# One pool for two projection stages, and smaller splitting steps for attention's weight tiles

## The chip, the cores and the metric

The kernel runs on one core of a Trainium2 chip. Its time is the device time of the whole program in microseconds; the number for a kernel is the median over its runs. A core has five instruction queues that run side by side: TensorE (PE, with its weight loads as PEld), VectorE (DVE), ScalarE (ACT), GpSimd (POOL) and SyncE (SP), the last of which only issues transfers here. Each queue is worked off in order. Whatever an instruction needs from another queue it waits for with a semaphore, and everything behind it on its own queue waits too.

## The reference

One decoder layer on a 1024 x 1024 input in float32: adaptive RMS norm, one wide input projection, a stick-breaking attention branch, a multi-scale causal pooling branch, two sigmoid gates that join them, and an output projection with a final norm.

```
h = rms_norm(x, norm_gain) * (1 + scale) + shift
q, k, v, z_a, u, z_b, m_a, m_b = split(h @ w_in)

z = q @ k.T * 64 ** -0.5                      # 16 heads of 64, s < t only
A[t, s] = sigmoid(z_ts) * prod over s < j < t of (1 - sigmoid(z_tj))
p_a = (concat_heads(A @ v) * silu(z_a)) @ w_branch_a
p_b = (pool(u) * silu(z_b)) @ w_branch_b

merged = sigmoid(m_a) * p_a + sigmoid(m_b) * p_b
out = rms_norm(x + gate * (merged @ w_out), final_gain)
```

## The kernel before

Every matrix product is made in three passes. An operand is split into a high half, the operand rounded to the type that PE reads (`F32R`), and a low half, the rest; the product is high x high, high x low and low x high, summed in one PSUM bank. The high half comes from a cast on ACT (`act.copy`), the low half from a subtraction on DVE or POOL. `h`, split and transposed, stays in SBUF as `hT` for the whole first part.

The stages follow each other on PE in this order: the pooling input `u`; the values `v` (tiles `vp`); the joining gate `m_b` (tiles `mp`); the gate of the pooling branch `z_b` (tiles `wzb`); the pooling branch's product (tiles `bp`); attention, in which the remaining projections (tiles `p`: k, q, z_a, m_a) are mixed with the heads' own work; and the last products (`pa`, `o`).

**Values and joining gate** are both made by `seven` (line 565 on), which forms a 2 x 2 block product from seven block products instead of eight, in the order p1, p5, p6, p7, p4, p3, p2, each of 48 matmuls. Its operands are weight blocks, loaded by the function that the caller hands in (line 679 for values, 697 for the gate), some of which are first added or subtracted on DVE: `a_s1` loads `a21` into a weight buffer and `a22` into a buffer of tag `ar`, adds them (line 576), loads `a11` into the other `ar` buffer and keeps the difference in `s2k` (line 578). `a_op` (lines 547 to 549) splits the result, `b_op` (lines 553 to 555) splits sums of `h` blocks into tiles of tag `bhl`. Banks are copied out by ACT (line 598) or added to by DVE (line 562). Finished values are split (lines 685 and 686) and stored to DRAM (line 687); finished gates go through a sigmoid (line 701) and are stored (line 702).

Tiles come out of pools. A tag is a ring of `bufs` buffers that all tiles of that tag share. `vs` and `ms` are two pools on the right side of SBUF, opened and closed one after the other, so `ms` lies on the bytes that `vs` had; the sizes of their last tags differ, so equal tags do not lie on equal bytes. `raw` and `whl` (the loaded and the split weights) are in the pool `wts`, which is open all the time and has two buffers of each.

**Attention** works on 64 units of one head and 256 queries. For a block row of queries PE makes the logits `z`, ACT writes `om` and `be` from them (two sigmoids, lines 921 and 922), POOL puts ones and zeros on the diagonal block of each (line 926), DVE runs a product scan along `om` (line 928) and multiplies it onto `be`. PE transposes blocks of `be` into a bank, ACT and DVE split them into `wt` (lines 947 and 948), and PE multiplies them with the values (`av`). Between these, PE works off the projection tiles: 32 weight tiles of 128 x 1024, each with 48 matmuls `p`. `load_parts` (line 138) loads and splits such a tile through `load_w` (line 127) and `split` (line 112): one cast of 128 x 1024 on ACT (line 121), and one subtraction of 128 x 1024 on POOL (line 116; on DVE for the tile number `MASKED`). Both of the two `raw` and `whl` buffers are in use, so a tile is split when the matmuls of the tile two before it are done. SP issues the loads of the tiles (line 129) in one queue with the moves of q and k between partitions (line 799) and the stores of attention's result (line 978).

What sets the order on the queues: PE's order from attention on is the order of the program (`pinned`), and so is that of some instructions on the other engines. All the rest is ordered by a planner when the program is built. It goes through a simulated run and issues whatever is ready on a free queue, earlier program lines first. In the pools with `reuse_waits="tile"` an instruction waits only for the tiles that lay on its own bytes.

Of the kernel before, what the change touches and what calls it, by code (L numbers as in the profile page):

```python
# [9 lines left out]
F32 = mybir.dt.float32  # L10
F32R = mybir.dt.float32r
AF = mybir.ActivationFunctionType
ALU = mybir.AluOpType
PSUM = bass.MemoryType.PSUM

P = 128
D = 1024
S = 1024
KB = D // P
# [17 lines left out]
MASKED = 4  # L37

HD = 64
# [12 lines left out]
def block_kernel(ctx, tc, a, out):  # L52
    nc = tc.nc
    v, act, gp = nc.vector, nc.scalar, nc.gpsimd

    def pool(name, **kw):
        return tc.tile_pool(name=name, bufs=1, reuse_waits="tile", **kw)
# [69 lines left out]
    def load_w(src, name, hi_eng, lo_eng):  # L127
        raw = wts.tile([P, KB, P], F32, tag="raw", bufs=2, name=name + "_raw")
        nc.sync.dma_start(raw.rearrange("p k c -> p (k c)"), src)
        return split(raw, [P, KB, P], wts, "whl", 2, hi_eng, lo_eng, name)  # L130
# [5 lines left out]
        tiles += [CK + p, CQ + p] + [gates.pop(0) for _ in range(GATES[p])] + [CZA + p]  # L136
    tiles += gates
    def load_parts(i, name):
        return load_w(a["w_in"][tiles[i]], name, act, v if i == MASKED else gp)

    def mm3(ps, whl, mhl, kbs, mov, first=True, last=True):
        (wh, wl), (mh, ml) = whl, mhl
# [38 lines left out]
    with pool("init") as init:  # L181
# [30 lines left out]
        def load(dst, src):  # L212
            tc.keep_in_program_order(nc.sync.dma_start(dst, src))
# [338 lines left out]
    def b_op(src, pl, bufs, name):  # L552
        hl = pl.tile([P, 2, 2, 512], F32R, tag="bhl", bufs=bufs, name=name)
        act.copy(hl[:, 0], src)
        v.tensor_sub(hl[:, 1], src, hl[:, 0].bitcast(F32))
        return lambda m, e: hl[:, m, e]

    def k2(t, q):
        return t[:, 2 * q:2 * q + 2]
# [4 lines left out]

    def seven(nm, sums, load, b_of, a_moves, ta, tb, final, direct):

        s2k = sums.tile([P, 4, 512], F32, name=nm + "s2k")

        def raw(first, m, k, q, name):
            t = (wts if first else sums).tile([P, 2, 512], F32, tag="raw" if first else "ar", bufs=2, name=f"{nm}{name}_{q}")  # L570
            load(t, m, k, q)
            return t

        def a_s1(q):
            r, w = raw(1, 1, 0, q, "a21"), raw(0, 1, 1, q, "a22")
            v.tensor_add(r, r, w)
            w = raw(0, 0, 0, q, "a11s")
            v.tensor_sub(k2(s2k, q), r, w)
            return r

        def a_s3(q):
            r, w = raw(1, 0, 0, q, "a11d"), raw(0, 1, 0, q, "a21d")
            v.tensor_sub(r, r, w)
            return r

        def a_s4(q):
            r = raw(1, 0, 1, q, "a12s")
            v.tensor_sub(r, r, k2(s2k, q))
            return r

        a_of = dict(
            p1=lambda q: raw(1, 0, 0, q, "a11"), p5=a_s1, p6=lambda q: k2(s2k, q), p7=a_s3,
            p4=lambda q: raw(1, 1, 1, q, "a22"), p3=a_s4, p2=lambda q: raw(1, 0, 1, q, "a12"),
        )

        def copied(tag, bufs, j, src):
            t = sums.tile([P, 512], F32, tag=tag, bufs=bufs, name=f"{nm}{tag}_{j}")
            act.copy(t, src)
            return t

        chain, keep = {}, {}
        for name in ("p1", "p5", "p6", "p7", "p4", "p3", "p2"):
            c = {"p5": "b", "p3": "b", "p2": "c"}.get(name, "a")
            if c not in chain:
                chain[c] = [bank((tb if c == "b" else ta)[j // 2], f"{nm}{name}_{j}") for j in range(4)]
            ps = chain[c]
            for q in range(2):
                al, bl = a_op(a_of[name](q), f"{nm}{name}a{q}"), b_of(name, q)
                for j in range(4):
                    js = slice(j * P, j * P + P)  # L610
                    for e in range(2):
                        for i, (w, m) in enumerate(((0, 0), (0, 1), (1, 0))):
                            l, r = (bl(m, e)[:, js], al[:, w, e]) if a_moves else (al[:, w, e, js], bl(m, e))
                            mm(
                                ps[j], l, r, start=name in ("p1", "p5", "p2") and (q, e, i) == (0, 0, 0),
                                stop=(q, e, i) == (1, 1, 2), skip_group_check=True,
                            )
            for j in range(4):
                if name == "p1":
                    keep["s1", j] = copied("s1", 4, j, ps[j])  # L620
                elif name == "p6":
                    keep["s2", j] = copied("s2", 4, j, ps[j])
                elif name == "p7":
                    final(1, 1, j, added(copied("s3", 4, j, ps[j]), chain["b"][j]))
                elif name == "p4":
                    final(1, 0, j, ps[j] if direct else copied("s3", 4, j + 4, ps[j]))
                elif name == "p3":
                    final(0, 1, j, added(keep["s2", j], ps[j]))
                elif name == "p2":
                    final(0, 0, j, added(keep["s1", j], ps[j]))  # L630

    with pool("vp") as vp:

        tq = [vp.tile([P, 4, 512], F32, name=f"ht{i}") for i in range(4)]

        def hq(k, n, q):
            sl = slice(4 * k + 2 * q, 4 * k + 2 * q + 2), slice(512 * n, 512 * n + 512)
            return [t[:, sl[0], sl[1]].bitcast(F32) for t in (h_hi, h_lo)]

        def difference(dst, x, y, name):  # L640
            tmp = vp.tile([P, 2, 512], F32, tag="tmp", bufs=1, name=name)
            v.tensor_sub(dst, x[0], y[0])
            v.tensor_sub(tmp, x[1], y[1])
            v.tensor_add(dst, dst, tmp)

        def without(dst, x, y):
            v.tensor_sub(dst, x[0], y)
            v.tensor_add(dst, dst, x[1])

        def make_t(i, q):  # L650
            dst = k2(tq[i], q)
            if i == 0:
                difference(dst, hq(0, 1, q), hq(0, 0, q), f"tmp0_{q}")
            elif i == 1:
                without(dst, hq(1, 1, q), k2(tq[0], q))
            elif i == 2:
                difference(dst, hq(1, 1, q), hq(0, 1, q), f"tmp2_{q}")
            else:
                without(dst, hq(1, 0, q), k2(tq[1], q))

        for i in reversed(range(KB)):
            ps = any_bank(f"u{i}_1")
            mm3(ps, whl[i], h, range(KB), hmov(1))
            use[i](1, ps)
            make_t((7 - i) // 2, (7 - i) % 2)
        early.close()

        def h_parts(nm, pl):
            def of(name, q):
                if name in ("p1", "p2", "p3"):  # L670
                    k, n = dict(p1=(0, 0), p2=(1, 0), p3=(1, 1))[name]
                    return lambda m, e: hT[:, m, 4 * k + 2 * q + e, 512 * n:512 * n + 512]
                return b_op(k2(tq[("p5", "p6", "p7", "p4").index(name)], q), pl, 2, f"{nm}{name}b{q}")
            return of

        with pool("vs", side="right") as vs:

            def load_v_w(t, m, k, q):
                nc.sync.dma_start(t.rearrange("p k c -> p (k c)"), a["w_v"][m, 2 * k + q])

            def values(m, n, j, src):
                sb = 4 * n + j
                vo = vs.tile([P, 8, 2, HD], F32R, tag="vo", bufs=3, name=f"vo{sb}_{m}")
                pv = src.rearrange("p (h d) -> p h d", d=HD)
                act.copy(vo[:, :, 0], pv)
                v.tensor_sub(vo[:, :, 1], pv, vo[:, :, 0].bitcast(F32))
                nc.sync.dma_start(
                    v_d[4 * m:4 * m + 4, :, sb].rearrange("n p c -> p n c"),
                    vo.rearrange("p (n h) i d -> p n (h i d)", h=2).bitcast(F32),
                )  # L690

            seven("v", vs, load_v_w, h_parts("v", vs), True, ("av", "tr"), ("pj", "z"), values, True)

        with pool("ms", side="right") as ms:

            def load_m_w(t, m, k, q):
                nc.sync.dma_start(t.rearrange("p k c -> p (k c)"), a["w_mb"][m, 2 * k + q])

            def gate_b(m, n, j, src):
                t = ms.tile([P, 512], F32, tag="go", bufs=3, name=f"sb{4 * m + j}_{n}")  # L700
                act.activation(t, src, AF.Sigmoid)
                nc.sync.dma_start(sb_d[4 * m + j][:, 512 * n:512 * n + 512], t)

            seven("m", ms, load_m_w, h_parts("m", ms), False, ("pj", "z"), ("av", "tr"), gate_b, True)

    turns[0] = cycle(("av", "tr", "pj", "z"))
    diffs = ExitStack()
# [500 lines left out]
```

## Time and profile before

| | |
|---|---|
| Runs | 1206.62, 1205.14, 1205.30 us; median 1205.3 |
| The profiled execution | 1206.08 us, of which its span is 1204.3 |
| PE busy | 1174.5 us (98%) |
| DVE busy | 861.4 us (72%) |
| ACT busy | 563.9 us (47%) |
| POOL busy | 241.6 us (20%) |
| Values (`vp`), in the chain of waits | 129.01 to 205.17 us |
| Joining gate (`mp`) | 205.17 to 289.44 us |
| Attention (first `p` to the last) | 453.24 to 1023 us |

A time in the profile counts from the start of the span. A group of the profile is read as line, engine, operation, names (out<-in), shape and count, then busy microseconds, nanoseconds of one, and the idle time of the engine before them with what ended it. In a timeline a row starts with its start and length, and the idle time of its engine before it stands in brackets. In a row of waits stand the sum, the count and the longest. A windows row gives start and end, length, the busy time and count of PE, PEld, DVE, ACT and POOL, and then the share of full clock that PE was granted, the share of the transfer engines and GB/s.

### The profile page before, as it was taken

The page shows a single profiled execution, that of the slowest core. Times are in us where ns is not written, and L with a number is a line of the kernel's source. Part 1 is how long each engine was busy: PE and PEld are TensorE (multiplying, and loading weights), DVE is VectorE, ACT ScalarE, POOL GpSimd, SP SyncE. Part 2 cuts the span into 40 slices and gives each one's busy share as a digit, 9 for nine tenths or more (in the row PEclk, how much of TensorE's full clock was granted, in tenths as well). Part 3 has the DMA queues.
Part 4 walks back from the last instruction along what each step waited for, and adds up shares of the span by engine and source line. Part 5 has one row for each costly group of instructions (what it writes and reads, how often), then busy time and mean ns, then how long its engine had stood idle before and what let it go on. Part 6 is the DMA issues. An engine that isn't in the chain of part 4 may idle for free.

```text
span 1204.3 us, 15853 instructions
## 1 busy us (share of the span) xinstructions
PE 1174.5 (98%) x5602; PEld 976.4 (81%) x5602; DVE 861.4 (72%) x1135; ACT 563.9 (47%) x1042; POOL 241.6 (20%) x376
## 2 busy tenths in 40 slices
PE   8999999899999999999999999999999999999997
PEld 7888888688888887887788878887878888888886
DVE  5767466554997651887888888879788885785643
ACT  5561363363223432656566566665656654232211
POOL 1000000000000003334343443435344441000001
PEclk9999999899999999999999999999999999999999
DMA  9652339546634357232323132422423115975612
GB/s 346 259 186 100 122 106 309 179 137 241 216 106 158 103 176 219 75 93 85 82 71 113 63 104 72 122 71 88 106 83 88 49 66 197 333 267 168 224 65 79
DMA packets 74753, 172.51 MB, mean 143 GB/s; under 512 B 9393, under 2 KB 22833, under 8 KB 72498
## 3 DMA queue, kind: packets, MB, share of 16 engines
q1 hardware_dynamic: 68770, 160.82, 40.9%
q10 hardware_dynamic: 5904, 10.68, 2.5%
q8 instruction: 44, 0.72, 0.2%
q14 instruction: 35, 0.29, 0.1%
HBM read 121.14 MB, written 33.56 MB: 128 GB/s over the span
## 4 chain that ended last, share of the span: by engine, by line
PE 81%; DVE 7%; issue 4%; DMA 4%; ACT 2%; POOL 1%; SPq 0%; POOLq 0%; ACTq 0%; DVEq 0%
PE p L101 21%; PE wzb L101 7%; PE pa L101 7%; PE bp L101 6%; PE o L101 6%; PE vp L101 6%; PE mp L101 5%; PE u L101 5%; PE z L101 4%; PE av L101 4%; PE wt L101 4%; DVE om L928 3%; PE ua L101 3%; PE wm L101 1%; DVE be L101 1%
## 5 line engine op out<-in xcount | busy, mean ns | idle before, releaser
L101 PE MATMUL p<-hT,w 128*128 128x512 f32 x1536 | 392.6, 392 | 0.0
L101 PEld LDWEIGHTS p<-hT,w 128*128 128x128 f32 x1536 | 283.0, 188 | 58.0 <-DVE klo L101 0.3
L928 DVE TENSOR_TENSOR_SCAN om<-om 128x512 f32<-128x512 f32 (+7 forms) x128 | 183.6, 1435 | 52.6 <-POOL om L926 27.4
L116 POOL TENSOR_TENSOR w<-w_raw,w 128x1024 fp32r<-128x1024 f32 x31 | 80.5, 2596 | 458.7 <-ACT w L121 453.6
L921 ACT ACTIVATE om<-z 128x512 f32<-128x512 f32 (+2 forms) x192 | 94.8, 493 | 130.6 <-PE z L101 99.3
L926 POOL TENSOR_SCALAR_AFFINE_SELECT om<-om 128x128 f32<-128x128 f32 x128 | 78.5, 613 | 182.2 <-ACT om L921 162.3
L948 DVE TENSOR_TENSOR wt<-wt,wt 128x512 fp32r<-128x512 f32 (+1 forms) x160 | 99.0, 620 | 20.8 <-ACT wt L947 20.3
L947 ACT CAST wt<-wt 128x512 fp32r<-128x512 f32 (+1 forms) x160 | 88.1, 551 | 46.8 <-PE wt L101 46.0
L101 PE MATMUL av<-wt,vv 128*128 128x512 f32 x320 | 106.0, 412 | 0.3 <-DVE wt L948 0.3
L101 PE MATMUL wt<-ident,be 128*128 128x128 f32 x576 | 90.8, 274 | 13.0 <-DVE wt L948 8.7
L101 DVE TENSOR_TENSOR be<-be,om 128x511 f32<-128x511 f32 (+7 forms) x128 | 101.1, 794 | 1.1
L922 ACT ACTIVATE be<-z 128x512 f32<-128x512 f32 (+2 forms) x192 | 94.1, 490 | 0.0
L101 PEld LDWEIGHTS wt<-ident,be 128*128 128x128 f32 x576 | 68.8, 140 | 30.1 <-DVE wt L948 9.3
L101 PE MATMUL pa<-ga,wa 128*128 128x512 f32 x384 | 89.6, 389 | 0.1
L101 PE MATMUL o<-wo,mhl 128*128 128x512 f32 (+1 forms) x408 | 89.6, 377 | 0.0
L101 PE MATMUL wzb<-hT,wzb 128*128 128x512 f32 x384 | 87.2, 389 | 0.0
L101 PEld LDWEIGHTS o<-wo,mhl 128*128 128x128 f32 x408 | 73.5, 188 | 14.1
L101 PEld LDWEIGHTS pa<-ga,wa 128*128 128x128 f32 x384 | 72.0, 188 | 15.4 <-DVE wa L116 0.5
L101 PEld LDWEIGHTS wzb<-hT,wzb 128*128 128x128 f32 x384 | 72.1, 188 | 15.0
L101 PE MATMUL z<-kl,q 128*128 128x512 f32 (+2 forms) x192 | 65.5, 341 | 0.0
L101 PE MATMUL z<-kh,q 128*128 128x512 f32 (+2 forms) x192 | 64.1, 334 | 1.3 <-DMA q<-qlo 1.3
L101 PE MATMUL u<-hT,wg 128*128 128x512 f32 x240 | 55.5, 391 | 0.0
(261 smaller groups left out, 1692.4 us busy)
## 6 DMA issues: line engine op xcount, KB each, us to landing
w_raw<-in_w_in SPq DMA_DIRECT2D x32, 512.0 KB, 3.5
v_d<-vo SPq DMA_DIRECT2D x16, 512.0 KB, 4.2
vv<-v_d SPq DMA_DIRECT2D x8, 1024.0 KB, 5.3
wa_raw<-in_w_branch_a SPq DMA_DIRECT2D x16, 512.0 KB, 4.6
wa<-in_w_mod SPq DMA_DIRECT2D x7, 1024.0 KB, 7.0
kh<-kh SPq DMA_DIRECT2D x48, 128.0 KB, 2.3
va<-in_w_v SPq DMA_DIRECT2D x10, 512.0 KB, 3.6
ma<-in_w_mb SPq DMA_DIRECT2D x10, 512.0 KB, 4.5
```

Source lines behind the costliest of these rows:

```text
L101: ins = op(*args, **kw)
L116: lo_eng.tensor_tensor(lo, src, hi.bitcast(F32), op=ALU.subtract)
L921: act.activation(om[:, b0:b0 + n], zp[:, :n], AF.Sigmoid, scale=-0.125)
L922: act.activation(be[:, b0:b0 + n], zp[:, :n], AF.Sigmoid, scale=0.125)
L926: gp.affine_select(out=tl[:, :P], in_=tl[:, :P], pattern=[[1, P]], compare_op=ALU.is_gt, fill=fill, base=0, channel_multiplier=-1)
L928: v.tensor_tensor_scan(om[:, :W], om[:, :W], om[:, :W], 1.0, ALU.mult, ALU.min)
L947: act.copy(wt[:, 0, :off], pt[:, :off])
L948: v.tensor_sub(wt[:, 1, :off], pt[:, :off], wt[:, 0, :off].bitcast(F32))
```

## The change

Values and joining gate take their tiles from one pool, `vs`, that stays open over both; `s2k` becomes a tag with one buffer that both use, the tags `ar`, `bhl`, `s1`, `s2` and `s3` are shared as they are, and the gate's output tiles `go` get buffers beside the values' `vo`. The pool closes behind the gate. The arithmetic of both stages is the same.

In attention, `load_parts` no longer calls `load_w` except for the masked tile. It casts a tile in two halves of 512 columns on ACT, and subtracts in four pieces of 256 columns on POOL. A piece depends on the half cast that it reads.

```diff
     def load_parts(i, name):
-        return load_w(a["w_in"][tiles[i]], name, act, v if i == MASKED else gp)
+        if i == MASKED:
+            return load_w(a["w_in"][tiles[i]], name, act, v)
+        raw = wts.tile([P, KB, P], F32, tag="raw", bufs=2, name=name + "_raw")
+        nc.sync.dma_start(raw.rearrange("p k c -> p (k c)"), a["w_in"][tiles[i]])
+        hl = wts.tile([P, 2, KB, P], F32R, tag="whl", bufs=2, name=name)
+        for e in range(2):
+            es = slice(4 * e, 4 * e + 4)
+            act.copy(hl[:, 0, es], raw[:, es])
+        for e in range(4):
+            es = slice(2 * e, 2 * e + 2)
+            gp.tensor_tensor(hl[:, 1, es], raw[:, es], hl[:, 0, es].bitcast(F32), op=ALU.subtract)
+        return hl[:, 0], hl[:, 1]
...
-        s2k = sums.tile([P, 4, 512], F32, name=nm + "s2k")
+        s2k = sums.tile([P, 4, 512], F32, tag="s2k", bufs=1, name=nm + "s2k")
...
-    with pool("vp") as vp:
+    with ExitStack() as vps:
+
+        vp = vps.enter_context(pool("vp"))
...
-        with pool("vs", side="right") as vs:
...
-            seven("v", vs, load_v_w, h_parts("v", vs), True, ("av", "tr"), ("pj", "z"), values, True)
-
-        with pool("ms", side="right") as ms:
...
-            seven("m", ms, load_m_w, h_parts("m", ms), False, ("pj", "z"), ("av", "tr"), gate_b, True)
+        vs = vps.enter_context(pool("vs", side="right"))
...
+        def gate_b(m, n, j, src):
+            t = vs.tile([P, 512], F32, tag="go", bufs=3, name=f"sb{4 * m + j}_{n}")
+            act.activation(t, src, AF.Sigmoid)
+            nc.sync.dma_start(sb_d[4 * m + j][:, 512 * n:512 * n + 512], t)
+
+        seven("v", vs, loads("w_v"), h_parts("v"), True, ("av", "tr"), ("pj", "z"), values, True)
+        seven("m", vs, loads("w_mb"), h_parts("m"), False, ("pj", "z"), ("av", "tr"), gate_b, True)
```

More of the change, by code (lines that the diff above doesn't have):

```diff
@@ L666, in block_kernel, with h_parts @@
         early.close()
-        def h_parts(nm, pl):
+        vs = vps.enter_context(pool("vs", side="right"))
+        def h_parts(nm):
             def of(name, q):
@@ L672, in of @@
                     return lambda m, e: hT[:, m, 4 * k + 2 * q + e, 512 * n:512 * n + 512]
-                return b_op(k2(tq[("p5", "p6", "p7", "p4").index(name)], q), pl, 2, f"{nm}{name}b{q}")
+                return b_op(k2(tq[("p5", "p6", "p7", "p4").index(name)], q), vs, 2, f"{nm}{name}b{q}")
             return of
-        with pool("vs", side="right") as vs:
[L678 to L690, printed above, removed]
-            seven("v", vs, load_v_w, h_parts("v", vs), True, ("av", "tr"), ("pj", "z"), values, True)
@@ L694, in block_kernel, with loads, load @@
-        with pool("ms", side="right") as ms:
[L696 to L702, printed above, removed]
-            seven("m", ms, load_m_w, h_parts("m", ms), False, ("pj", "z"), ("av", "tr"), gate_b, True)
+        def loads(w):
+            def load(t, m, k, q):
+                nc.sync.dma_start(t.rearrange("p k c -> p (k c)"), a[w][m, 2 * k + q])
+            return load
@@ new lines, in values @@
+        def values(m, n, j, src):
+            sb = 4 * n + j
+            vo = vs.tile([P, 8, 2, HD], F32R, tag="vo", bufs=3, name=f"vo{sb}_{m}")
+            pv = src.rearrange("p (h d) -> p h d", d=HD)
+            act.copy(vo[:, :, 0], pv)
+            v.tensor_sub(vo[:, :, 1], pv, vo[:, :, 0].bitcast(F32))
+            nc.sync.dma_start(
+                v_d[4 * m:4 * m + 4, :, sb].rearrange("n p c -> p n c"),
+                vo.rearrange("p (n h) i d -> p n (h i d)", h=2).bitcast(F32),
+            )
```

## The prediction, made before the changed kernel was run

> **What bounds the kernel now.** I read the page first (busy time by engine), then what PE waited for, then the chain of waits, and then the timeline at the places that these name. Busy time and PE's waits, summed by releaser:
>
> ```profile
> PE 1174.5 (98%) x5602; PEld 976.4 (81%) x5602; DVE 861.4 (72%) x1135; ACT 563.9 (47%) x1042; POOL 241.6 (20%) x376
> PE wt L101 <- DVE wt L948: 8.7, 9, 1.8
> PE mp L101 <- ACT mp5a L548: 3.9, 1, 3.9
> PE wt L101 <- POOL tp L977: 2.2, 3, 1.1
> PE wt L101 <- DVE be L101: 1.9, 4, 0.6
> PE mp L101 <- DVE mp6b L555: 0.8, 1, 0.8
> ```
>
> TensorE is the bound, so only what lets PE run denser can gain. Two places come into the change's reach: the transposes of attention (`wt`, 8.7 + 2.2 + 1.9 = 12.8 us) and the start of the joining gate (`mp`). The chain of waits gives the second its full size:
>
> ```profile
> 129.01 76.16 PE vp L101 x336
> 205.17 4.38 PE mp L101 x20
> 209.55 7.99 DMA ma<-in_w_mb
> 289.44 87.04 PE wzb L101 x384
> ```
>
> The values stage and the gate stage each run 336 matmuls of one size. The first takes 76.16 us without a break; the second runs from 205.17 to 289.44, which is 84.27 us. The difference, **8.1 us**, is what the gate stage loses, and the chain passes there through a transfer of `ma`. The timeline of that place:
>
> ```profile
> 207.65 0.34 SPq L697 DMA_DIRECT2D ma<-in_w_mb  x1
> 208.25 1.25 SPq L687 DMA_DIRECT2D v_d<-vo  x2
> 209.55 1.28 SPq L697 DMA_DIRECT2D ma<-in_w_mb  x1
> ...
> 217.64 1.23 DVE L576 TENSOR_TENSOR ma<-ma,ma 128x1024 f32<-128x1024 f32 x1 [0.52 <-DMA ma<-in_w_mb]
> 218.90 1.04 ACT L548 CAST mp5a<-ma 128x1024 fp32r<-128x1024 f32 x1 [1.76 <-DVE ma L576]
> 220.00 1.22 PE L101 MATMUL mp<-mp5b,mp5a 128*128 128x512 f32 x2 [3.95 <-ACT mp5a L548]
> ```
>
> The addend of the second product (the `ar` tile of line 576) is asked for at 209.55, the first thing behind the last store of values. It lands 7.99 us later, with two stores and another load in front of it; then add, cast, and PE has been idle for 3.95 us. The idle time has a second price:
>
> ```profile
> 219.20:225.90 6.70, 5.91 (x14) 4.65 (x15) 4.21 (x4) 1.79 (x2) 0.00 (x0) 0.50 0.82 287
> L101 PE MATMUL mp<-mp5b,mp5a 128*128 128x512 f32 x14 | 6.2, 631 | 3.9 <-ACT mp5a L548 3.9
> ```
>
> Behind the gap the granted clock is 0.50, and 14 matmuls take 6.2 us instead of 14 x 76.16/336 = 3.2. So the 8.1 us are 4 of waiting, 3 of half clock, and 0.8 at `mp6b` with small change. The Trainium skill ("TensorE: Matmul & The Clock Gate", Part 1) has the clock halved after an idle window of about 3.4 us; the trace agrees, since 3.95 us of idling drew it. By that rule a remnant of the gap under 3.4 us would cost its own length alone.
>
> **Part one: one pool.** No arithmetic is added or removed. Today the first tiles of a new pool come behind the last instruction on the old one, whatever bytes they need. Two rows show the same at the next change of pool, and two how the values stage starts:
>
> ```profile
> 288.19 3.76 SPq L702 DMA_DIRECT2D sb_d<-sb  x4
> 293.09 0.42 SPq L526 DMA_DIRECT2D u<-u_d  x1
> 99.33 0.33 SPq L679 DMA_DIRECT2D va<-in_w_v  x1
> 139.73 1.52 PE L101 MATMUL vp<-vp5a,vp5b 128*128 128x512 f32 x6
> ```
>
> The first load of the pooling branch stands behind the last four stores of the gate. The values stage had its `ar` load at 99.33, and its second product starts at 139.73 with no idle time. With one pool `ar` is the same two buffers for both stages, and values is done with them by the end of its fourth product of seven, at 129.0 + 4 x 76.16/7 = 172.5 at the latest. Both loads of the gate's second product (`a22`, `a11s`) can therefore go out in the middle of values. They move past the stores of values on SP; each keeps SP 0.3 to 0.4 us. What is late next? The other half, `a21`, goes into a shared weight buffer; its second block leaves at 207.65 as today and lands at about 212, while PE wants it at 205.0 + 11.0 + 5.5 = 221.5. The `bhl` casts, behind the copies of the first product today, become free too. Bounds: 0, when the planner leaves the loads where they are, and 8.1, when the stage runs like values. I take **8.1**, since the neighbour with the same code and free buffers shows it. The gate's own output tiles add 6 KB beside the `vo` tiles, and `s2k` is one buffer, last read in values' sixth product; neither has a wait near the path.
>
> **Part two: smaller casts and subtractions.** Per weight tile of attention one cast of 1024 columns becomes two of 512, and (30 tiles; one goes to DVE) one subtraction becomes four of 256. The rows by form:
>
> ```profile
> L116 POOL TENSOR_TENSOR w<-w_raw,w 128x1024 fp32r<-128x1024 f32 x31 | 80.5, 2596 | 458.7 <-ACT w L121 453.6 <-DMA kh<-kh 5.1
> L977 POOL TENSOR_TENSOR tp<-tp,za 128x256 f32<-128x256 f32 x32 | 27.6, 862 | 75.1 <-DVE tp L974 75.1
> L121 ACT CAST w<-w_raw 128x1024 fp32r<-128x1024 f32 x32 | 33.6, 1050 | 8.9 <-PE bp L101 8.9
> L887 ACT CAST ga<-gr 128x512 fp32r<-128x512 f32 x16 | 9.8, 621 | 22.3 <-DMA gr<-ga_d 21.6 <-ACT wt L947 0.5
> 449.07 2.41 POOL L116 TENSOR_TENSOR w<-w_raw,w 128x1024 fp32r<-128x1024 f32 x1 [380.79 <-ACT w L121]
> 453.24 1.10 PE L101 MATMUL p<-hT,w 128*128 128x512 f32 x4
> SPq L129 <- POOL w L116: 77.1, 11, 17.7
> ```
>
> `tp` is the same operation on 256 columns: 4 x 0.862 = 3.45 us against 2.60, so POOL works 0.85 us longer per tile, 26 us in all; ACT 2 x 0.621 - 1.050 = 0.19 us, 6 in all. The subtractions can begin after the first half cast, 0.43 us earlier, so a tile is done about 0.4 us later. What hides it is the matmuls of the tile before. The tightest case is the first tile, done at 451.48 with its matmuls at 453.24: 1.8 us of cover, so no price. SP, too, waits for the last subtraction before it refills `raw` (77.1 us), with the moves of q and k queued behind: 0.4 us more in waits of up to 17.7, costed at nothing.
>
> The gain lies between POOL and DVE:
>
> ```profile
> 583.40 2.39 POOL L116 TENSOR_TENSOR w<-w_raw,w 128x1024 fp32r<-128x1024 f32 x1 [1.33 <-ACT w L121]
> 583.70 3.43 DVE L928 TENSOR_TENSOR_SCAN om<-om 128x640 f32<-128x640 f32 x1 [2.03 <-ACT om L921]
> 587.06 0.66 DVE L948 TENSOR_TENSOR wt<-wt,wt 128x512 fp32r<-128x512 f32 x1
> 587.78 0.66 PE L101 MATMUL wt<-ident,be 128*128 128x128 f32 x4 [1.79 <-DVE wt L948]
> 600.90 1.49 DVE L928 TENSOR_TENSOR_SCAN om<-om 128x640 f32<-128x640 f32 x1 [0.83 <-ACT om L921]
> 507.83 2.75 DVE L101 TENSOR_TENSOR be<-be,om 128x511 f32<-128x511 f32 x1
> 999.68 2.47 DVE L888 TENSOR_TENSOR ga<-gr,ga 128x512 fp32r<-128x512 f32 x1 [1.65 <-ACT ga L887]
> ```
>
> A scan of 640 columns takes 1.49 us alone and 3.43 when it starts inside a subtraction: it ends one scan after the subtraction does. The low half behind it is late, and PE stands 1.79 us. I count ten DVE instructions stretched like this between 507.83 and 999.68. The Trainium skill ("SBUF — State Buffer", SBUF: two separate sides) calls the port that GpSimd shares with a VectorE instruction of two SBUF inputs an exclusive lock for a whole instruction; the row agrees. With pieces of 0.86 us DVE waits at most 0.86, on average half of that, where it waited 1.94.
>
> The bounds for PE: at best the 12.8 us of `wt` waits shrink by the 8.0 that I find in PE's gaps within 9 us behind those ten; gaps without a lock in front stay. At worst the selects of `om`, which stand behind the subtraction on POOL, come later by 0.85 us a tile, which is the slower rival. I take **3.0**: the gaps directly behind a lock, less what selects 0.4 us later give back, and less that the planner lays out POOL, ACT and DVE anew.
>
> **Sum.** The profiled execution took 1206.08 us (span 1204.3 and 1.8 around it): 1206.1 - 8.1 - 3.0 = 1195.0. The median of the runs is 0.8 lower, so **1194.2**.
>
> **Rivals.** *The loads stay behind the stores* (the change does not do what it says): the values-to-gate gap remains and only attention gains, 1205.3 - 3.0 = 1202.3. For it speaks that a planner sets SP's order; against it, that loads into buffers already shared (207.65) do pass stores today. *The gate gains, attention pays back what it gains and 3 us more*: 1205.3 - 8.1 + 3.0 = 1200.2; for it, that every queue is laid out anew. *Attention keeps nothing of the ten gaps*: 1205.3 - 8.1 - 8.0 = 1189.2.
>
> *Slower: POOL becomes late for the scans.* Rows that speak for it:
>
> ```profile
> 546.48 0.30 POOL L926 TENSOR_SCALAR_AFFINE_SELECT om<-om 128x128 f32<-128x128 f32 x1
> 546.81 2.36 DVE L928 TENSOR_TENSOR_SCAN om<-om 128x1024 f32<-128x1024 f32 x1 [4.57 <-POOL om L926]
> 546.97 2.29 POOL L926 TENSOR_SCALAR_AFFINE_SELECT om<-om 128x128 f32<-128x128 f32 x1
> ```
>
> The select at 546.48 went off the moment a subtraction ended (24 of 31 do), DVE had stood 4.57 us for it, and the next select, 0.30 by itself, took 2.29 under the scan. Four pieces can be held up so four times. With 0.85 us per tile on 24 tiles, passed on to PE as at 583.70 (1.79 of 1.94), that is 24 x 0.85 x 0.92 = 18.8 us: 1205.3 - 8.1 + 18.8 = 1216.0. It decides for slower from 8.1/24 = 0.34 us per tile. Against it: PE lost nothing near 546.81, and a DVE instruction that slips between two pieces had to run before the select's scan anyway. The skill's page on SBUF says that whoever starts first blocks the other; by that alone this rival would be the likelier.
>
> **How the numbers follow.** Forecast 1194.2 (1191 to 1198 by itself): 0.60. Attention pays back, 1200.2: 0.15. Ten gaps gone, 1189.2: 0.08. Loads stay, 1202.3: 0.07. Slower, 1205.5 to 1216: 0.10. About 0.2% (2.4 us) is what a measurement of this kernel can tell from no change. Faster takes the forecast, 0.08, nearly all of 0.15 and half of 0.07: 0.85; within 0.2% 0.06; slower 0.09. The range 1189 to 1203 leaves the slower case out.
>
> **What would show it.** In the changed profile an `ma` load well before 192; `mp` following `vp` without PE's wait on `mp5a`, no 0.50 of clock near 220, and the gate's 336 matmuls in about 76 us. Subtractions on POOL of 0.7 to 0.9 us, no scan of 640 columns above 2.4, and PE's `wt` waits near 10 us. A gap left at `mp5a`, or `wt` waits above 16, would make the prediction wrong.

## The result, and the profile after

The changed kernel takes **1193.97 us** (median of 4 runs, 1193.47 to 1195.88) against 1205.96 for the kernel before (4 runs, 1205.14 to 1206.87): a ratio of **0.9901, 95% interval 0.9888 to 0.9915**. Forecast were 1194.2, in a range of 1189 to 1203. The profiled execution took 1195.88 us (span 1194.2), the highest of the four, so the trace shows 10.2 us of the 12.0 that the medians differ by. Two single executions further down, of 1561 us (the split alone) and 2393 us (the kernel before), fell into a slower state, and the medians given there leave them out.

Where the 10.2 us came from, by the first instruction of each stage on PE (us):

| stage on PE | before | after | difference | forecast |
|---|---|---|---|---|
| up to values | 128.85 | 128.43 | -0.42 | 0 |
| values `vp` | 76.16 | 76.16 | 0 | 0 |
| joining gate `mp` | 84.27 | 78.03 | **-6.24** | -8.1 |
| `wzb` and `bp` | 163.96 | 163.96 | 0 | 0 |
| attention, first `p` to first `pa` | 569.79 | 566.25 | **-3.54** | -3.0 |
| the rest | 181.3 | 181.3 | 0 | 0 |

The first row is no effect of the change: up to there the code is the same, and the kernels below, which share it too, begin values between 127.84 and 130.52 us.

The page of the changed kernel, its busy line, and PE's waits, summed by releaser (sum, count, longest):

```profile
PE 1169.7 (98%) x5602; PEld 973.9 (82%) x5602; DVE 852.4 (71%) x1135; ACT 566.1 (47%) x1073; POOL 264.6 (22%) x469
PE wt L101 <- DVE wt L957: 7.9, 9, 1.7
PE wt L101 <- POOL tp L986: 1.7, 3, 0.7
PE mp L101 <- DVE mp6b L566: 1.5, 1, 1.5
PE wt L101 <- DVE be L101: 1.4, 3, 0.6
```

The 3.9 us at `mp5a` are gone from the list; `mp6b` went from 0.8 to 1.5; the three `wt` rows went from 12.8 to 11.0. POOL works 23.0 us more (forecast 26), ACT 2.2 (forecast 6). The chain of waits at the two stages:

```profile
201.69 4.77 DMA ma<-in_w_mb
211.21 7.80 DMA ma11s<-in_w_mb
221.49 4.92 DMA ma11d<-in_w_mb
228.95 53.83 PE mp L101 x236
```

It still passes through transfers between 201 and 229, but other ones. The timeline of the changed kernel there (start, length; in brackets the engine's idle time before):

```profile
145.35 0.33 SPq L693 DMA_DIRECT2D ma<-in_w_mb  x1
148.63 0.33 SPq L693 DMA_DIRECT2D ma11s<-in_w_mb  x1
...
206.48 1.23 DVE L587 TENSOR_TENSOR ma<-ma,ma 128x1024 f32<-128x1024 f32 x1 [1.01 <-DMA ma<-in_w_mb]
208.23 1.21 DVE L560 TENSOR_TENSOR mp1a<-ma,mp1a 128x1024 fp32r<-128x1024 f32 x1
215.47 11.04 PE L101 MATMUL mp<-mp5b,mp5a 128*128 128x512 f32 x48
216.60 1.23 DVE L587 TENSOR_TENSOR ma<-ma,ma 128x1024 f32<-128x1024 f32 x1 [3.68 <-DMA ma<-in_w_mb]
219.10 1.22 DVE L589 TENSOR_TENSOR ms2k<-ma,ma11s 128x1024 f32<-128x1024 f32 x1 [1.28 <-DMA ma11s<-in_w_mb]
226.54 1.22 DVE L594 TENSOR_TENSOR ma11d<-ma11d,ma21d 128x1024 f32<-128x1024 f32 x1 [1.25 <-DMA ma11d<-in_w_mb]
227.68 1.22 DVE L566 TENSOR_TENSOR mp6b<-ht,mp6b 128x1024 fp32r<-128x1024 f32 x1
228.95 3.28 PE L101 MATMUL mp<-mp6b,mp6a 128*128 128x512 f32 x13 [1.53 <-DVE mp6b L566]
```

The first `a22` and `a11s` leave at 145.35 and 148.63, in the middle of values, where the same loads left at 209.55 and 210.89 before. The 48 matmuls of the second product run from 215.47 without idle time. What is left is one wait of 1.53 us at 228.95, and its chain runs through the second blocks. The second `a21` block is added only at 216.60. The difference behind it on DVE stands until 219.10 for the second `a11s` block, which left at 211.21 and took 7.80 us. The subtraction after that gives the weight buffer back at 221.5, so `ma11d` leaves at 221.49 and takes 4.92 us, and the difference at 226.54 stands on DVE in front of the subtraction that PE needs. The windows view over the second product and the rest of the stage shows full clock (the column behind PE's busy time and count):

```profile
215.47:226.35 10.88, 10.88 (x49) 1.00 0.77 272
226.35:282.62 56.27, 54.74 (x241) 1.00 0.42 141
```

The gap of 1.53 us drew no half clock, which agrees with the idle window of about 3.4 us that the Trainium skill ("TensorE: Matmul & The Clock Gate", Part 1) gives. In two kernels below, gaps of 2.05 and 2.46 us did draw one (last section).

In attention, the groups by form and the counterpart of the stretched scan at 583.70 of before:

```profile
L149 POOL TENSOR_TENSOR w<-w_raw,w 128x256 fp32r<-128x256 f32 x124 | 106.7, 892 | 442.4 <-ACT w L146 442.4
L146 ACT CAST w<-w_raw 128x512 fp32r<-128x512 f32 x62 | 35.4, 624 | 8.8 <-PE bp L101 8.8
575.86 4.00 POOL L149 TENSOR_TENSOR w<-w_raw,w 128x256 fp32r<-128x256 f32 x4 [0.90 <-ACT w L146]
576.68 1.96 DVE L937 TENSOR_TENSOR_SCAN om<-om 128x640 f32<-128x640 f32 x1 [2.12 <-POOL w L149]
579.28 0.66 PE L101 MATMUL wt<-ident,be 128*128 128x128 f32 x4 [0.39 <-DVE wt L957]
```

The scan of 640 columns takes 1.96 us where it took 3.43, and PE stands 0.39 us where it stood 1.79. Below, the **stretch** of a kernel is the sum over its trace of what DVE instructions that start inside one of these subtractions take above the median of the same shape outside of them, counted from 0.2 us on. It was 13.3 us before and is 3.9 now, with no instruction held up by more than 0.50. The windows over attention (length; PE busy and count; clock), before and after:

```profile
453.24:1023.03 569.79, 555.17 (x2818) 1.00 0.33 97
```

```profile
446.58:1012.83 566.25, 554.23 (x2817) 1.00 0.34 97
```

Of the 3.5 us, 2.6 are idle time of PE (14.6 to 12.0). The other 0.9 lie in the matmuls' own recorded time and are not put down to anything here.

### The profile page after: what moved, and what is told of

It is laid out like the page before. It is cut to its first block, busy times and chain, and to the rows that moved or that the text cites. A ratio compares the mean times of both kernels' runs of the same rounds, so it can differ in the third digit from the quotient of the medians.

```text
span 1194.2 us, 15986 instructions
## 1 busy us (share of the span) xinstructions
PE 1169.7 (98%) x5602; PEld 973.9 (82%) x5602; DVE 852.4 (71%) x1135; ACT 566.1 (47%) x1073; POOL 264.6 (22%) x469
## 4 chain that ended last, share of the span: by engine, by line
PE 80%; DVE 7%; DMA 4%; issue 4%; POOL 2%; ACT 2%; SPq 0%; POOLq 0%; ACTq 0%; DVEq 0%
PE p L101 22%; PE wzb L101 7%; PE pa L101 7%; PE bp L101 6%; PE o L101 6%; PE vp L101 6%; PE u L101 5%; PE mp L101 5%; PE av L101 4%; PE wt L101 4%; PE z L101 4%; DVE om L937 3%; PE ua L101 2%; POOL w L149 1%; DVE be L101 1%
## 5 line engine op out<-in xcount | busy, mean ns | idle before, releaser
L937 DVE TENSOR_TENSOR_SCAN om<-om 128x512 f32<-128x512 f32 (+7 forms) x128 | 178.6, 1396 | 55.7 <-POOL om L935 30.7
L149 POOL TENSOR_TENSOR w<-w_raw,w 128x256 fp32r<-128x256 f32 x124 | 106.7, 892 | 442.4 <-ACT w L146 442.4
L935 POOL TENSOR_SCALAR_AFFINE_SELECT om<-om 128x128 f32<-128x128 f32 x128 | 74.8, 584 | 174.0 <-ACT om L930 157.8
L101 DVE TENSOR_TENSOR be<-be,om 128x511 f32<-128x511 f32 (+7 forms) x128 | 98.7, 776 | 1.0
```

Of the source, the lines that this page charges most:

```text
L101: ins = op(*args, **kw)
L149: gp.tensor_tensor(hl[:, 1, es], raw[:, es], hl[:, 0, es].bitcast(F32), op=ALU.subtract)
L935: gp.affine_select(out=tl[:, :P], in_=tl[:, :P], pattern=[[1, P]], compare_op=ALU.is_gt, fill=fill, base=0, channel_multiplier=-1)
L937: v.tensor_tensor_scan(om[:, :W], om[:, :W], om[:, :W], 1.0, ALU.mult, ALU.min)
```

## The experiments

The two theories under test. *Gate:* with one pool the planner may put the gate's first addend loads into the middle of values; the rivals are that the place of the buffers mattered, and that what is left is due to the crowd of transfers. *Attention:* long subtractions on POOL block DVE, and shorter ones let it in; one rival is that the earlier start behind a half cast helps, another that the planner's new order on DVE does; the price is that POOL gets done later.

### Each part alone

The kernel before with one pool, and `load_parts` as it was:

```diff
-        with pool("vs", side="right") as vs:
+        vs = vps.enter_context(pool("vs", side="right"))
...
-        with pool("ms", side="right") as ms:
```

> The kernel before with one pool for values and gate, weight tiles split as before. If the two parts act apart from each other, this keeps the gate stage's gain of the changed kernel, 84.3 to 78.0 us, and nothing of attention's: 1206.0 - 6.2 = 1199.8 us. If the gate's gain needed the finer splitting, it is 1203 or more.

Measured: 1197.88 us (6 runs) against 1206.30, ratio 0.9939 [0.9919, 0.9959]. The kernel before with the two casts and four subtractions alone:

```diff
-        return load_w(a["w_in"][tiles[i]], name, act, v if i == MASKED else gp)
+        for e in range(2):
+            act.copy(hl[:, 0, 4 * e:4 * e + 4], raw[:, 4 * e:4 * e + 4])
+        for e in range(4):
+            gp.tensor_tensor(hl[:, 1, 2 * e:2 * e + 2], ...)
```

> The kernel before with the two casts and four subtractions alone. If the parts add up, attention takes 566.3 instead of 569.8 us and the rest is as before, the gate stage at 84.3: 1202.4 us. If attention's gain came from its earlier start or another order behind the one pool, it is 1206.

Measured: 1202.52 us (11 runs), ratio 0.9969 [0.9958, 0.9981]; attention 565.84 us. The two gains, 8.4 and 3.8 us, add up to 12.2; together the parts brought 12.0. So each works on its own stage, and neither is seen to feed the other. In the joined pool's trace the gate stage has no wait of PE at all, and attention is where it was (569.66 us):

```profile
145.54 0.33 SPq L682 DMA_DIRECT2D ma<-in_w_mb  x1
226.43 5.76 PE L101 MATMUL mp<-mp6b,mp6a 128*128 128x512 f32 x23
204.67:281.21 76.54, 76.50 (x338) 1.00 0.53 179
```

The gate takes 76.54 us, 7.7 less than before. Here the second `a21` block was added at 214.30, 2.3 us earlier than in the whole change, the difference that waits for `a11s` began at 218.14, 1.0 us earlier, and the wait at `mp6b` is not there.

### Is it the bytes or the pool?

The kernel before, with two pools, but with the gate's output tiles as large as the values', so that each tag of the second pool lies on the bytes of the same tag of the first:

```diff
-                t = ms.tile([P, 512], F32, tag="go", bufs=3, ...)
+                t = ms.tile([P, 2, 512], F32, tag="go", bufs=3, ...)[:, 0]
```

> The kernel before with two pools, but the gate's output tiles padded to the size of the values' tiles, so that every tag of the second pool lies on the bytes of the same tag of the first. If the planner puts a new pool's first tiles behind the last instruction of the old pool whatever bytes they need, the loads stay behind the stores of values and nothing changes: 1206 us, gate stage 84 us. If the loss came from unequal tags lying on each other's bytes, it goes away: 1199.8 us.

Measured: 1207.1 us (12 runs), ratio 1.0004 [0.9989, 1.0019]. The load stays behind the last stores of values, and PE's gap with it:

```profile
208.09 2.13 SPq L687 DMA_DIRECT2D v_d<-vo  x2
210.27 0.95 SPq L697 DMA_DIRECT2D ma<-in_w_mb  x1
220.27 3.35 PE L101 MATMUL mp<-mp5b,mp5a 128*128 128x512 f32 x7 [4.38 <-ACT mp5a L548]
```

The `ar` buffers were free here as early as in the joined pool and on the same bytes; what held the load all the same is that a new pool's first tile comes behind the old pool's last instruction. So the rival of the bytes falls. That the pool is the cause rests on this and on the joined pool alone, whose one edit moved the load; by which rule the planner does it was not looked at.

### What the gate stage still loses

The changed kernel with four `ar` buffers for values and gate:

```diff
-tag="raw" if first else "ar", bufs=2
+tag="raw" if first else "ar", bufs=2 if first or nm == "b" else 4
```

> The changed kernel with four instead of two buffers of tag ar for values and gate, so that the second block's two loads can go out early too. The changed kernel's rest of a loss in the gate stage (78.0 against 76.2 us) hangs on the second load of a21, which leaves at 209.5 and takes 7 us among other loads and stores. If it is the crowd, with two loads fewer it lands about 2 us earlier, PE's wait of 1.5 us on mp6b shrinks, and the time is 1192.5 us. If it is the order on VectorE alone (the add in front of the subtraction that frees the weight buffer), it stays at 1194.0 us.

Measured: 1193.79 us (5 runs), ratio 0.9902 [0.9885, 0.9919]. Its trace has the gate at 76.48 us, without the wait at `mp6b`, though for neither of the reasons expected. The second `a21` block is as late as in the changed kernel; what is gone is DVE's wait for the second `a11s` block right behind it:

```profile
216.58 1.22 DVE L587 TENSOR_TENSOR ma<-ma,ma 128x1024 f32<-128x1024 f32 x1 [3.42 <-DMA ma<-in_w_mb]
217.84 1.23 DVE L589 TENSOR_TENSOR ms2k<-ma,ma11s 128x1024 f32<-128x1024 f32 x1
```

But the median is the changed kernel's within 0.2 us, so the trace of one execution says more than the runs bear out. Therefore the changed kernel was run once more, for a second trace:

> The changed kernel itself, a second time, for a second trace of its gate stage. In the first trace that stage took 78.03 us, of which 1.53 is one wait of PE at mp6b, behind an a21 block that landed at 216.48 us; the same stage took 76.5 us in the two kernels that had the joined pool and no such wait. Theory A (the wait is there in every execution, a term of the sum that was forecast 1.9 us too high): the gate again takes 77.5 to 78.5 us and the median is 1195 to 1196. Theory B (the block lands on the edge, and the wait comes and goes from one execution to the next): the gate takes about 76.5 us where the block lands early enough, and the median stays at 1193.5 to 1194.2, as in the three unprofiled runs.

Measured: 1194.08 us (6 runs, 1192.69 to 1200.81). The profiled execution was the 1200.81, with a granted clock of 0.947 in place of 0.999. Its values took 76.16 us all the same, but attention took 2.9 us and `wzb` and `bp` 1.4 us more than in the first trace, so only its gate stage is used here. It takes 77.43 us, with a wait at `mp6b` of 0.96, between the two theories; the median is the one of theory B. Another kernel below, whose code is the changed kernel's up to attention, has the stage at 76.50 us with no wait. So the wait is neither fixed nor absent: it was 1.53, 0.96 and 0 us in three executions of the same instructions. Last, the block that came late gets buffers of its own, beside the four `ar`:

```diff
-            r, w = raw(1, 1, 0, q, "a21"), raw(0, 1, 1, q, "a22")
+            if nm == "m":
+                r = sums.tile([P, 2, 512], F32, tag="ae", bufs=2, name=f"{nm}a21_{q}")
+                load(r, 1, 0, q)
+                w = raw(0, 1, 1, q, "a22")
```

> The changed kernel with four buffers for the addends of values and joining gate and with a buffer pair of its own for the gate's a21 blocks, so that all loads of the gate's second product can go out while values runs. If the second a21 block (issued at 209.47, landed at 216.48 in the changed kernel) is all that the gate stage still loses, the stage takes 76.2 us, no wait at mp5a or mp6b, and the time is 0 to 1.5 us under the changed kernel's: 1192.5 to 1193.8. If the crowd on the DMA queues behind values is the cause, the ma11d block lands late all the same, and the stage stays at 77 to 78 us.

Measured: 1192.95 us (4 runs, 1192.66 to 1194.03), ratio 0.9898 [0.9878, 0.9918]. The stage takes 76.16 us, what values took before, at full clock and without a wait:

```profile
213.20 1.23 DVE L599 TENSOR_TENSOR ma11d<-ma11d,ma21d 128x1024 f32<-128x1024 f32 x1 [3.01 <-DMA ma11d<-in_w_mb]
204.03:280.19 76.16, 76.16 (x337) 1.00 0.43 141
```

The difference of the second `ma11d` is done at 214.4 instead of 227.8. So with all loads of the second product early nothing of the stage's loss is left; four `ar` buffers alone had left 0.3 us of it in their one trace. The 1.0 us in the medians is less than a measurement of this kernel tells from no change, so that the faster version is faster is shown by the stage, not by the time.

### Two casts, four subtractions: which of them?

Two casts and one subtraction, on the kernel before:

```diff
+        for e in range(2):
+            act.copy(hl[:, 0, 4 * e:4 * e + 4], raw[:, 4 * e:4 * e + 4])
+        gp.tensor_tensor(hl[:, 1], ...)
```

> The kernel before with the cast of attention's weight tiles in two halves, and the subtraction whole. If the lock between GpSimd and VectorE is what the finer splitting relieves, this relieves nothing: VectorE instructions are still stretched by up to 2 us, 1206 us (205 to 207). If the gain is an accident of queues laid out anew, this can have it too: 1202 to 1204 us.

Measured: 1206.15 us (12 runs), ratio 1.0009 [0.9999, 1.0019]; attention 570.44 us. The other way round:

```diff
+        act.copy(hl[:, 0], raw)
+        for e in range(4):
+            gp.tensor_tensor(hl[:, 1, 2 * e:2 * e + 2], ...)
```

> The kernel before with one whole cast and four subtractions of 256 columns. By the lock, the whole gain of attention is here: 1202.4 us, and no VectorE instruction stretched by more than 0.8 us. By the queues laid out anew, anything between 1202 and 1207 us.

Measured: 1204.57 us (12 runs), ratio 0.9989 [0.998, 0.9998]; attention 569.02 us. The lock alone does not explain the gain: the stretch fell from 13.3 to 3.5 us, somewhat further than with the whole split (4.1), and yet attention won 0.8 us and not 3.9. PE's waits of this kernel, and the timeline of a place where one goes back to POOL:

```profile
PE wt L101 <- DVE wt L959: 7.0, 8, 1.6
PE wt L101 <- POOL tp L988: 3.5, 3, 1.9
PE wt L101 <- POOL w L149: 1.3, 1, 1.3
562.15 5.50 POOL L149 TENSOR_TENSOR w<-w_raw,w 128x256 fp32r<-128x256 f32 x4 [0.25 <-ACT w L146]
567.60 0.29 POOL L937 TENSOR_SCALAR_AFFINE_SELECT om<-om 128x128 f32<-128x128 f32 x1
567.92 2.09 DVE L939 TENSOR_TENSOR_SCAN om<-om 128x896 f32<-128x896 f32 x1 [1.11 <-POOL om L937]
570.54 0.72 POOL L988 TENSOR_TENSOR tp<-tp,za 128x256 f32<-128x256 f32 x1 [2.41 <-DVE tp L985]
571.33 0.52 PE L101 MATMUL wt<-ident,be 128*128 128x128 f32 x3 [1.87 <-POOL tp L988]
```

Before, the waits on POOL were 2.2 us in all; here they are 4.8. The four pieces begin when the whole cast is done and last until 567.65; the select stood behind them, DVE stood 1.11 us for the select, and PE 1.87 for what follows. At the same place of the kernel before PE waits 0.39 us, in the changed kernel 0.61. So a second price stands beside the lock: **how late POOL is done with a tile**.

### Eight pieces, and no subtraction at all

Two casts with eight subtractions of 128 columns, on the kernel before:

```diff
+        for e in range(8):
+            gp.tensor_tensor(hl[:, 1, e:e + 1], raw[:, e:e + 1], ...)
```

> The kernel before with two casts and eight subtractions of 128 columns. By the lock VectorE waits at most about 0.4 us, half as long as with four, and GpSimd works longer: 1202.4 us, give or take 1, the same as four. If GpSimd's lateness for the scans weighs, it is above 1204 us.

Measured: 1205.73 us (11 runs), ratio 1.0001 [0.9992, 1.001]; attention 569.02 us. A piece takes 564 ns, a tile 4.51 us on POOL, and the stretch is down to 0.9. The waits on DVE shrink, and those on POOL take their place:

```profile
PE wt L101 <- DVE wt L959: 5.5, 5, 1.9
PE wt L101 <- POOL tp L988: 5.1, 5, 2.5
569.99 0.63 PE L101 MATMUL wt<-ident,be 128*128 128x128 f32 x3 [2.46 <-POOL tp L988]
L149 POOL TENSOR_TENSOR w<-w_raw,w 128x128 fp32r<-128x128 f32 x248 | 130.8, 564 | 446.3 <-ACT w L146 446.3
```

The longest of these waits costs more than its length: from 570.26 on, PE is granted half clock for 3.41 us, which takes up to 1.7 us more of attention.

Then the bound of what attention could win. In the kernel before, with one cast, the subtraction is replaced by an instruction that only writes; this leaves out the low half of 31 of attention's weight tiles, which are zero instead.

```diff
-            gp.tensor_tensor(hl[:, 1, es], raw[:, es], hl[:, 0, es].bitcast(F32), op=ALU.subtract)
+        gp.memset(hl[:, 1].bitcast(F32), 0.0)
```

> The kernel before with a GpSimd fill of zeros in place of attention's subtractions; the low half of the weights is left out of the result. A fill reads nothing from SBUF. If the stretched VectorE instructions come from GpSimd reading SBUF, none is stretched and attention gains at least what the four pieces gained: 1199 to 1202.4 us. If they come from GpSimd being busy at all, or do not matter for PE, it stays at 1204 to 1206 us.

Measured: 1195.38 us (5 runs), ratio 0.9908 [0.9892, 0.9923], a gain of 10.1, more than was expected by any theory.

```profile
L147 POOL MEMSET w<- 128x1024 f32 x31 | 29.6, 954 | 432.9 <-PE bp L101 384.8 <-PE p L101 48.0
L937 DVE TENSOR_TENSOR_SCAN om<-om 128x640 f32<-128x640 f32 x16 | 23.9, 1492 | 8.3 <-ACT om L930 7.9 <-POOL be L935 0.2
PE wt L101 <- DVE wt L957: 5.5, 7, 1.0
454.90:1013.36 558.46, 552.52 (x2817) 1.00 0.34 98
```

It takes both prices away: no DVE instruction is stretched (the 16 scans of 640 columns take 1.49 us on average, as one does alone), and POOL is done in 0.95 us without waiting for a cast, so no wait on POOL is left. PE idles 5.9 us in attention instead of 14.6. Attention is 11.3 us shorter; the other 2.6 us lie in the matmuls' own recorded time, and no run here explains them. The Trainium skill ("SBUF — State Buffer", SBUF: two separate sides) has DVE instructions with two SBUF inputs contend only with a GpSimd operation that reads SBUF; the trace agrees, as these instructions of 954 ns, which read nothing there, stretched none.

### Two pieces

With two prices the best number of pieces need not be four. The changed kernel with two subtractions of 512 columns, each behind its half cast:

```diff
-        for e in range(4):
-            es = slice(2 * e, 2 * e + 2)
+        for e in range(2):
+            es = slice(4 * e, 4 * e + 4)
```

> The changed kernel with two subtractions of 512 columns per weight tile instead of four of 256, each behind its own half cast. Theory of two prices: a tile is done at (first cast + all subtractions) after the cast began, 0.62 + 2 x 1.3 = 3.2 us, where it was 1.05 + 2.60 = 3.65 before, 4.19 with four pieces, 4.63 with one cast and four pieces, 5.13 with eight; each us of it costs attention about 6.5 us, and each us by which DVE instructions are stretched under a subtraction (13.4 before, 4.0 with four pieces) costs 0.8. Two pieces then stretch DVE by some 6 to 9 us in all but are done 0.4 us earlier than before, so attention takes 562 to 564 us and the kernel 1190 to 1192, 2 to 4 us under the changed kernel. Rival, the lock alone (smaller pieces gain by what they free DVE of, and lateness costs little): two pieces stand between one and four, attention 567 to 568.5 us and the kernel 1195 to 1197, 1 to 3 us above the changed kernel.

Measured: 1193.39 us (4 runs, 1191.4 to 1193.62), ratio 0.9895 [0.9871, 0.9918]. Attention takes 564.5 us, 1.7 less than with four pieces: outside the 567 to 568.5 of the lock alone, and 0.5 above what the two prices gave; a piece takes 1.54 us and not the 1.3 put in. The time lies between the two ranges expected, 1.4 us above the one of the two prices.

```profile
L149 POOL TENSOR_TENSOR w<-w_raw,w 128x512 fp32r<-128x512 f32 x62 | 94.0, 1536 | 445.3 <-ACT w L146 445.3
PE wt L101 <- DVE wt L957: 6.7, 7, 1.4
PE wt L101 <- POOL tp L986: 1.0, 2, 0.6
445.09:1009.63 564.54, 554.50 (x2818) 1.00 0.34 98
```

All forms side by side. "Done" is one cast plus all pieces, from the rows of their means; the last column is an estimate: it takes 8.4 us of attention for each us of "done" and 0.91 for each us of stretch, sizes set by the second and the fourth row against the first.

| casts x pieces | done, us | stretch, us | PE waits on POOL, us | attention, us | by two prices |
|---|---|---|---|---|---|
| 1 x 1 (before) | 1.05 + 2.60 = 3.65 | 13.3 | 2.2 | 569.8 | |
| 1 x 4 | 1.05 + 4 x 0.894 = 4.63 | 3.5 | 4.8 | 569.0 | (set) |
| 2 x 1 | 2 x 0.62 + 2.59 = 3.83 | 11.0 | 2.4 | 570.4 | 569.2 |
| 2 x 4 (two pools) | 0.62 + 4 x 0.889 = 4.18 | 4.1 | 2.6 | 565.8 | (set) |
| 2 x 8 | 0.62 + 8 x 0.564 = 5.13 | 0.9 | 5.1 | 569.0 | 570.9 |
| 2 x 2 | 0.62 + 2 x 1.536 = 3.69 | 7.4 | 1.0 | 564.5 | 564.8 |

Two sizes bring the three other rows to within 1.9 us, where all rows lie within 6 us; the worst is that of eight pieces, which holds the half clock besides. That both prices exist is shown at single places (the scan at 583.70 before, the wait at 571.33 above) and borne out by the pairs (1 x 4 against 2 x 4: nearly the same stretch, 0.45 us later, 3.2 us longer; 1 x 1 against 2 x 2: as early, 5.9 us less stretch, 5.3 us shorter). How large they are is less sure. PE's order is the same in all these kernels, but the planner gave DVE another order in attention than before in each of the five others, and no run here holds that order still; nor is it shown that the prices are straight lines.

### The two best together

The early `a21` blocks and four `ar` buffers, with two subtractions of 512 columns.

> The two gains together: the early a21 loads of all_early (four addend buffers, a21 buffers of their own) and the two subtractions of 512 columns of two_subs. If the two parts are independent, as the joined pool alone (8.5 us) and the split alone (3.6 us) were, whose sum 12.1 is what the whole change brought, the gate takes 76.2 us (all_early), attention 564 to 565 us (two_subs), and the time is 1.0 us under all_early for the unprofiled runs: 1191 to 1192.3. If attention's gain hangs on what its first loads meet, which come at another time, the time is that of all_early, 1192.6 to 1194.0.

Measured: 1192.52 us (4 runs, 1192.19 to 1193.0), ratio 0.9897 [0.9869, 0.9924], the lowest of all, 1.5 us under the changed kernel. The stages are those of the parts (gate 76.16, attention 564.85), and the time lies between the two ranges expected, 0.2 above the first. Again the stages show it, while the runs alone could not tell it from no change.

## Why the prediction was right, and where it was off

- **The place of the gate's loads: right.** They leave at 145.35 and 148.63, well before 192, and there is no wait on `mp5a` and no half clock near 220. That a new pool, not the bytes, had held them is shown by the kernel with equal bytes and by the joined pool alone. The aside that a gap under 3.4 us "would cost its own length alone" fails: a gap of 2.05 us in the split alone was followed by 3.41 us of half clock.
- **"The stage runs like values", 8.1 us: the mechanism right, the size 0.3 to 1.9 us too large.** It was 6.2 and 6.8 us in two traces of the changed kernel and 7.7 with the joined pool alone. The step that fell short is "Both loads of the gate's second product (`a22`, `a11s`) can therefore go out in the middle of values". This holds for the first blocks. The second `a22` and `a11s` need the same two `ar` buffers, which DVE gives back only after the first sum (206.48) and the first difference (209.96), so the second `a11s` left at 211.21 and landed at 219.01. The question "what is late next?" was asked of the second `a21` block. That one left at 209.47 and not at 207.65, and landed at 216.48 and not at 212, but still before the 221.5 at which PE wants it; with four `ar` buffers it is as late, and that trace has no wait. That a transfer takes 7 to 8 us there could be read from the prediction's own row, 7.99 us for `ma` at 209.55. With all these loads early the stage does run like values, 76.16.
- **Attention, 3.0 us: close (3.5 in the trace, 3.8 in the medians of the split alone), with one reason of two missing.** The pieces of 0.86 us are 0.89, on 31 tiles and not 30, as the row shown there has it; no scan of 640 columns is above 1.97; the `wt` waits came to 11.0 where "near 10" stood. "A tile is done about 0.4 us later" is right (4.19 against 3.65 gives 0.5), and "what selects 0.4 us later give back" was in the sum, without a size. By the two prices above, an estimate, the lock gave about 8.5 us and the lateness took 4.5. That the half cast, as half of the change, is what keeps the lateness small enough was not seen: without it the gain is 0.8 us in the trace and 0.9 in the time.
- **What was costed at nothing: right.** PE waits nowhere for the subtraction of the tile that it multiplies next, and SP's longer wait before refilling `raw` shows in no wait of PE (its one wait for a move of q went from 1.3 to 0.8 us).
- **The rival "attention keeps nothing of the ten gaps"** (8.0 us) had a bound a little too low: with neither lock nor lateness PE idles 8.7 us less, and attention is 11.3 us shorter. None of the forms with pieces came near it; from two pieces on, each step that takes stretch away makes POOL later.
- **The slower rival, POOL late for the scans,** names a mechanism that is there, priced too high. It took 0.92 us of PE per us and tile, on 24 tiles: 22 us per us. The estimate from the runs is about 8, and the lock's gain stands against it. Its own mark of 0.34 us per tile was passed (0.5), and the kernel became faster; even eight pieces, 1.5 us later per tile, came out even with the kernel before (1.0001), not slower. The Trainium skill ("SBUF — State Buffer", SBUF: two separate sides) has whoever starts first block the other, and the traces agree for the single instruction: a scan of 640 columns took 3.43 us behind a subtraction, a select 2.29 under a scan. It does not say which of the two is late for PE, and that decided.
- **The sum.** Forecast were 11.1 us under 1205.3; measured were 12.0 under 1205.96. The trace of the changed kernel accounts for 6.24 + 3.54 + 0.42 = 10.2, its execution being 1.9 above the median; the two parts measured alone account for 8.4 + 3.8 = 12.2. The gate term was 0.3 to 1.9 us too large and the attention term 0.5 to 0.8 too small. That the time itself was hit to 0.2 us, from a base that moved by 0.7 us between the measurements, is luck.

## What to carry to other kernels

A wait for the first load of a stage can come from where its pool was opened, while the bytes are long free: look in the timeline at what the load stands behind, and open the pool a stage earlier. Cutting a GpSimd operation into pieces frees DVE and makes everything behind it on POOL later; count both, start the pieces behind half of what they read, and take the fewest pieces that do, here two. When a load is moved out of the way, ask of every further block that shares its buffers when the last reader gives them back; the place on the queue is not enough.

## What the runs showed of the hardware beyond that

A gap on PE had a second price, a stretch of half clock, and this came in two lengths, 3.41 and 6.83 us. Here are the 6.70 us behind the gap at `mp5a` in two of the kernels above (window; PE busy and count; granted clock), each from its own windows view. Eight pieces, with a gap of 3.34 us:

```profile
219.08:225.78 6.70, 6.70 (x23) 0.77 0.85 310
```

One cast and four pieces, 3.72 us:

```profile
219.66:226.36 6.70, 6.70 (x17) 0.54 0.90 301
```

At full clock 6.70 us hold 30 matmuls of 0.227 us. By the same view the gaps of 3.34, 3.38 and 3.60 us (eight pieces, the split alone, the write-only kernel) have clocks of 0.77, 0.76 and 0.75 behind them, some 1.5 us of loss beside the gap; those of 3.72 to 4.38 us (one cast and four pieces, two casts and one, before, equal bytes) have 0.54 to 0.58, some 2.6 to 2.9 us; and the 1.53 us of the changed kernel cost nothing more.

The length of the gap alone does not decide. In the split alone a gap of 2.05 us at `mp6b` (232.32 to 234.37) was followed by half clock from 235.58 to 238.99, and with eight pieces one of 2.46 us in attention by half clock from 570.26 to 573.67. A gap of 2.29 us in the write-only kernel (235.02 to 237.30) was followed by none. The traces fit a count in windows of 3.413 us on a fixed grid: the two half clocks of the split alone begin 17.07 us apart, 5 windows, and those with eight pieces 351.57 us, 103 windows. Counted on that grid from values to the last products, every window at full clock in which PE idled 2.05 us or more was followed by half clock, and none in which it idled 1.80 us or less; the 2.29 us fall into two windows, 0.92 and 1.37 us. Half clock went on for a second window where PE had idled 0.61 us or more in the first, and ended where it had idled 0.39 us or less. What lies between these figures no run here shows. So the 3.4 us that the Trainium skill ("TensorE: Matmul & The Clock Gate", Part 1) gives for the idle window agree with the length of the window here; the idle time that was enough within it is less.

A subtraction of 1024 columns takes GpSimd 2.60 us, and the pieces 2 x 1.54 = 3.07, 4 x 0.89 = 3.57 and 8 x 0.56 = 4.51 us: from four pieces to eight each further piece costs about 0.24 us, and the first halving 0.47, part of which is DVE getting in between. The operation `tp`, from whose 0.862 us the pieces were priced, was a good guide.
